# Attention with a running minimum, GpSimd adding the halves of pf, and evictions of 256 columns

## The chip, the cores and the metric

The kernel runs on one core of a Trainium2 chip. The metric is the device time of one execution in microseconds (us). A core has TensorE (PE; PEld is its weight load), VectorE (DVE), ScalarE (ACT), GpSimd (POOL) and SyncE (SP), which here issues nearly all DMA. Each works through its own instructions in order and waits on semaphores.

## The reference

One layer of a hybrid decoder on x of shape (1, 2048, 1024): an RMS norm, one input projection, three parallel branches (forgetting attention with 8 heads of 64, a Mamba-2 scan, a Griffin recurrence), each with a gate, and one output projection that is added to x. The change lies in the attention and in the output projection:

```python
q = rms_norm(q, q_g); k = rms_norm(k, k_g)
c = jnp.cumsum(log_f, axis=1)                       # per head
logits = einsum('bhqd,bhkd->bhqk', q_i, kt) * 64**-0.5 + (c_i[..., None] - ck[:, :, None, :])
logits = jnp.where(kpos[None, :] <= qpos[:, None], logits, -jnp.inf)
p = jax.nn.softmax(logits, axis=-1)
o = einsum('bhqk,bhkd->bhqd', p, vt)
...
mix = concatenate([y_att, y_ssd, y_lru], axis=-1)   # 512 + 1024 + 512
h = h + einsum('bse,ed->bsd', mix, w_out[l])
```

## The kernel before

All products are made of float32 values split into a high and a low part (names ending in h and l): three products of the parts, or two where one operand carries both parts in its 128 rows.

Up to about 1260 us the kernel normalises x, makes the projections and runs the state space and recurrent branches; q, k, v and the gates go to DRAM. In `group` p of q and k, line 804 scales q by the column `qg` of the constants `cv`, which line 294 multiplies by 0.125.

Then comes the attention. Its work is cut into 64 units (h, sb): a head and a block of 256 queries (two query tiles of 128). The heads 0 and 7 run sb from 7 down to 0, the others up. A unit has two halves:

- `logits` (L829 to L878): for each query tile and each chunk of up to 512 keys two products into S (L854, L855), then one VectorE instruction (L856) that writes L = S - cb, where cb is the cumulative sum of the keys, and keeps a running maximum mx. For the last chunk cb is replaced by cm, a masked copy that GpSimd makes (L849, two buffers). Then L859 negates mx on VectorE, and L860 is ScalarE's exp with bias mx, which also sums into sm. The page shows L856 as a custom instruction and a read of its accumulator, of 128x1.
- `attend` (L880 to L937): transposes T of L (L909), ScalarE's cast ph of T (L916), VectorE's remainder pl (L917), products O with v (L895, L896). v holds its two parts side by side, so O has two halves of 64 rows that must be added: O is copied to os (L929), transposed into pf (L933), and L934 on VectorE adds the halves of pf into ats, which is then multiplied by the gate zg (L935, GpSimd) and stored in at_d (L936). ats, os, zg have two buffers each; O and pf share two PSUM buffers.

The loop at the end interleaves the units: while unit i is attended, the logits of unit i + 1 are made. At every eighth unit (its third) the next but one head's keys, values and sums are loaded (`load_head`: cb 1 MB, kh twice 0.5 MB, vv 1 MB).

Between these, `fill` lets a generator `sweeps` run some steps as filler for TensorE. It makes the output projection in four sweeps over 16 row blocks t, two halves n of 512 columns each: `mix` loads the branch's block mt (L961, L963), casts it to mh (L964, ScalarE) and makes the remainder ml (L965, GpSimd); `half` makes 12 products into po (L977 to L979, four steps of three) and adds po to xr (L981, L983, VectorE). In the first two sweeps xr is loaded from x or from the partial sums pt_d (L996) and stored there again (L998), with two buffers; in the last two, xo takes its place. Before the first unit is attended, 12 steps of filler (three halves) are taken at once, after the logits of the first unit have been written (L1027 to L1033). During the attention po has one PSUM buffer; after it, from about 1920 us, five, and only the rest of the sweeps is left.

The order of the instructions on each engine is not that of the code: a scheduler arranges it by dependences and priorities. The logits of the first unit stand under `high_priority` and `issue_after`, which bring them up among the last projections.

Of the kernel before, what the change touches and what calls it, by code (L numbers as in the profile page):

```python
# [8 lines left out]
F32 = mybir.dt.float32  # L9
# [3 lines left out]
AF = mybir.ActivationFunctionType  # L13
ALU = mybir.AluOpType
AX = mybir.AxisListType
# [3 lines left out]
P = 128  # L19
# [11 lines left out]
FIRST = 12  # L31
# [16 lines left out]
def hybrid_block(ctx, tc, x, norm_g, w_in, q_norm_g, k_norm_g, forget_b, ssd_conv_w, ssd_conv_b,  # L48
# [8 lines left out]
    V, A, G, T = nc.vector, nc.scalar, nc.gpsimd, nc.tensor  # L57
# [142 lines left out]
    with tpool(name="p0", bufs=2) as p0, tpool(name="p01", bufs=1) as p01, \  # L200
# [71 lines left out]
        for tb in range(4):  # L272
            if tb + AHEAD < 4:
                norm_x(tb + AHEAD)
            for k in range(KD):
                pt, tag = ((psY, "Y"), (pst, "pt"))[(tb * KD + k) % 5 % 2]
                pt = pt.tile([P, 512], F32, name=f"pu{tb}_{k}", tag=tag)
                for i in range(4):
                    T.transpose(pt[:, i * P:(i + 1) * P],
                                xts[tb * 4 + i][:, k * P:(k + 1) * P], ident)  # L280
                g = ngc[:, k:k + 1]
                A.activation(uh[tb][k], pt, AF.Copy, scale=g)
                V.scalar_tensor_tensor(ul[tb][k], pt, g, uh[tb][k].bitcast(F32),
                                       op0=ALU.mult, op1=ALU.subtract)
            if tb == 0:
                pr = psY.tile([P, P], F32, name="pr2", tag="Y")
                T.transpose(pr, rows, ident)
                V.tensor_copy(cv, pr[:, 0:NV])


                j = CV["cw"]
                V.tensor_scalar(cv[:, j:j + 60], cv[:, j:j + 60], 0.5, None, op0=ALU.mult)
                j = CV["qg"]
                V.tensor_scalar(cv[:, j:j + 1], cv[:, j:j + 1], 0.125, None, op0=ALU.mult)
                j = CV["ba"]
                V.tensor_scalar(cv[:, j:j + 4], cv[:, j:j + 4], -1.0, None, op0=ALU.mult)
                j = CV["bx"]
                V.tensor_scalar(cv[:, j:j + 4], cv[:, j:j + 4], 0.5, None, op0=ALU.mult)
# [530 lines left out]
    def logits(h, sb):  # L829

        sm = a2.tile([P, 2], F32, name=f"sm{h}_{sb}", tag="sm")
        u = {"L": [], "sm": sm}
        steps = []

        def chunk(i, c0):
            kh, vv, cb, qh, ql = heads[h]
            u["vv"] = vv
            qt = sb * 2 + i
            n = (qt + 1) * P
            w = min(512, n - c0)  # L840
            if c0 == 0:
                u["L"].append(a4.tile([P, S], F32, name=f"L{h}_{qt}", tag="L"))
                u["mx"] = am.tile([P, 1], F32, name=f"mx{h}_{qt}", tag="mx")
            lt, mx = u["L"][i], u["mx"]
            last = c0 + w == n
            cc = cb[:, c0:c0 + w]
            if last:
                cm = a2.tile([P, 512], F32, name=f"cm{h}_{qt}", tag="cm")
                G.affine_select(out=cm[:, 0:w], in_=cc, pattern=[[-1, w]], compare_op=ALU.is_ge,  # L849
                                fill=-NEG, base=w - P, channel_multiplier=1)  # L850
                cc = cm[:, 0:w]
            qs = slice((sb % 2) * 256 + i * P, (sb % 2) * 256 + i * P + P)
            ps = psS.tile([P, 512], F32, name=f"S{h}_{qt}_{c0}", tag="S")
            T.matmul(ps[:, 0:w], qh[:, qs], kh[:, c0:c0 + w], start=True, stop=False)  # L854
            T.matmul(ps[:, 0:w], ql[:, qs], kh[:, c0:c0 + w], start=False, stop=True)  # L855
            V.tensor_tensor_reduce(lt[:, c0:c0 + w], ps[:, 0:w], cc, 1.0,  # L856
                                   -3.0e38 if c0 == 0 else mx, ALU.subtract, ALU.max, mx)
            if last:
                V.tensor_scalar(mx, mx, -1.0, None, op0=ALU.mult)  # L859
                A.activation(lt[:, 0:n], lt[:, 0:n], AF.Exp, bias=mx, accum_out=sm[:, i:i + 1])  # L860

        def first():
            j = units.index((h, sb))
            if j % 2 == 0 and j > 0:
                load_q(h, sb)
            za = a2.tile([P, 2, 64], F32, name=f"za{h}_{sb}", tag="za")
            u["za"] = za
            p, b = divmod(h, 2)
            dma(za, za_d[p][sb * 256:(sb + 1) * 256, b * 64:b * 64 + 64].rearrange(
                "(t p) c -> p t c", p=P))  # L870
            if j % 8 == 2 and h < 7:
                load_head(h + 1)

        steps.append(first)
        for i in range(2):
            for c0 in range(0, (sb * 2 + i + 1) * P, 512):
                steps.append(lambda i=i, c0=c0: chunk(i, c0))
        return u, steps  # L878

    def attend(h, sb, u, steps, fill):  # L880

        L, sm, vv, za = u["L"], u["sm"], u["vv"], u["za"]
        V.reciprocal(sm, sm)
        zg = a2.tile([P, 2, 64], F32, name=f"zg{h}_{sb}", tag="zg")
        for i in range(2):
            G.tensor_scalar(zg[:, i, :], za[:, i, :], sm[:, i:i + 1], None,
                            op0=ALU.mult)
        po = psO.tile([P, 256], F32, name=f"O{h}_{sb}", tag="O")
        nk = sb * 2 + 2

        def av(kp, ph, pl):
            for jj in range(2):
                kt = kp * 2 + jj
                ca = slice(P, 256) if kt == nk - 1 else slice(0, 256)
                T.matmul(po[:, ca], vv[:, kt, :], ph[:, jj, ca], start=(kt == 0), stop=False)  # L895
                T.matmul(po[:, ca], vv[:, kt, :], pl[:, jj, ca], start=False, stop=(kt == nk - 1))  # L896

        todo = None
        done = 0
        for kp in range(sb + 1):  # L900
            pt = psT.tile([P, 2, 256], F32, name=f"T{h}_{sb}_{kp}", tag="T")
            last = kp == sb
            ins = None
            for jj in range(2):
                kt = kp * 2 + jj
                for i in range(2):
                    if last and jj == 1 and i == 0:
                        continue
                    ins = T.transpose(pt[:, jj, i * P:(i + 1) * P], L[i][:, kt * P:(kt + 1) * P],  # L909
                                      ident)  # L910
            ph = a3.tile([P, 2, 256], F32R, name=f"ph{h}_{sb}_{kp}", tag="ph")
            pl = a3.tile([P, 2, 256], F32R, name=f"pl{h}_{sb}_{kp}", tag="pl")
            parts = [(slice(0, 2), slice(0, 256))] if not last else [
                (0, slice(0, 256)), (1, slice(P, 256))]
            for ja, ca in parts:
                A.copy(ph[:, ja, ca], pt[:, ja, ca])  # L916
                V.tensor_tensor(pl[:, ja, ca], pt[:, ja, ca], ph[:, ja, ca].bitcast(F32),  # L917
                                op=ALU.subtract)
            upto = len(steps) * (kp + 1) // (sb + 1)
            for st in steps[done:upto]:  # L920
                st()
            done = upto
            if todo is not None:
                av(*todo)
            todo = (kp, ph, pl)
            fill(ins)
        av(*todo)
        os_ = a2.tile([P, 256], F32, name=f"os{h}_{sb}", tag="os")
        A.copy(os_, po)  # L929
        pf = psO.tile([P, 256], F32, name=f"pf{h}_{sb}", tag="O")  # L930
        ats = a2.tile([P, 2, 64], F32, name=f"ats{h}_{sb}", tag="ats")
        for i in range(2):
            T.transpose(pf[:, i * P:(i + 1) * P], os_[:, i * P:(i + 1) * P], ident)  # L933
        V.tensor_reduce(ats, pf.rearrange("p (i u c) -> p i c u", i=2, u=2), axis=AX.X, op=ALU.add)  # L934
        G.tensor_tensor(ats, ats, zg, op=ALU.mult)  # L935
        dma(at_d[sb * 256:(sb + 1) * 256, h * 64:(h + 1) * 64].rearrange("(i p) c -> p i c", p=P),  # L936
            ats)  # L937
# [30 lines left out]
    def half(t, n, i, parts, xr):  # L968
# [5 lines left out]
        for j in range(4):  # L974
# [2 lines left out]
            T.matmul(ps, mh[:, j, :], h, start=(j == 0), stop=False)  # L977
            T.matmul(ps, mh[:, j, :], l, start=False, stop=False)  # L978
            T.matmul(ps, ml[:, j, :], h, start=False, stop=(j == 3))  # L979
        if kind in (0, 1):  # L980
            V.scalar_tensor_tensor(xr, ps, rsn[:, t, kind:kind + 1], xr, op0=ALU.mult, op1=ALU.add)  # L981
        else:
            V.tensor_tensor(xr, xr, ps, op=ALU.add)  # L983

    SEQ = ((12, "lru"), (8, 1), (4, 0), (0, "att"))

    def sweeps():
# [22 lines left out]
        for w, (t, i) in enumerate(work):  # L1010
# [13 lines left out]
                    dma(of[tsl, cs], xs[t][:, cs])  # L1024
            cur = nxt

    with tc.high_priority(offset=HP), tc.issue_after(anchor[1].ins):  # L1027
        cur, steps = logits(*units[0])
        for st in steps:
            st()  # L1030
    filler = sweeps()
    for _ in range(FIRST):
        next(filler)  # L1033
    count = [0, FIRST]
    recent = []

# [48 lines left out]
```

## Time and profile before

| what | value |
|---|---|
| median of 3 runs | 2093.52 us (2092.03 to 2095.52) |
| the profiled execution | 2093.96 us, span 2092.3 us |
| mean granted clock of TensorE | 0.986 |
| memory read, written | 168.22 MB, 94.57 MB |

In the rows of the profile, `out<-in` gives the tiles that an instruction writes and reads, L856 the line of the code. "busy" is the time in which an engine worked, "idle before" the time it stood still just ahead of these instructions, with what ended it behind the arrow. A row of waits reads "who waited <- for whom: us in total, times, longest". PEclk is the share of full speed at which TensorE's clock ran.

### The profile page before, as it was taken

The page shows a single profiled execution, that of the slowest core. Times are in us where ns is not written, and L with a number is a line of the kernel's source. Part 1 is how long each engine was busy: PE and PEld are TensorE (multiplying, and loading weights), DVE is VectorE, ACT ScalarE, POOL GpSimd, SP SyncE. Part 2 cuts the span into 40 slices and gives each one's busy share as a digit, 9 for nine tenths or more (in the row PEclk, how much of TensorE's full clock was granted, in tenths as well). Part 3 has the DMA queues.
Part 4 walks back from the last instruction along what each step waited for, and adds up shares of the span by engine and source line. Part 5 has one row for each costly group of instructions (what it writes and reads, how often), then busy time and mean ns, then how long its engine had stood idle before and what let it go on. Part 6 is the DMA issues. An engine that isn't in the chain of part 4 may idle for free. (4 is left out here: it accounts for less than half of the span.)

```text
span 2092.3 us, 35912 instructions
## 1 busy us (share of the span) xinstructions
PE 2008.3 (96%) x12485; PEld 1760.1 (84%) x12485; DVE 1261.7 (60%) x2720; ACT 956.7 (46%) x1989; POOL 540.6 (26%) x750
## 2 busy tenths in 40 slices
PE   7999999999999999998999998999999999999999
PEld 6788888887789998887888997978888888888887
DVE  6655555488874216767576255767777776884333
ACT  7444443466642214554444234555656555563010
POOL 0000001355531005454552001232223322212110
PEclk9999999999999999999999999999999999999999
DMA  5122233111123225666666647466466456342443
GB/s 195 41 71 61 71 112 96 39 42 42 42 72 95 83 81 161 189 186 201 193 163 177 163 147 218 135 175 164 128 178 187 126 151 155 116 142 78 136 137 120
DMA packets 287318, 265.18 MB, mean 127 GB/s; under 512 B 59780, under 2 KB 227232, under 8 KB 285088
## 3 DMA queue, kind: packets, MB, share of 16 engines
q1 hardware_dynamic: 286976, 262.85, 43.2%
q8 instruction: 99, 1.62, 0.3%
q14 instruction: 83, 0.68, 0.1%
q0 software_dynamic: 160, 0.03, 0.1%
HBM read 168.22 MB, written 94.57 MB: 126 GB/s over the span
## 5 line engine op out<-in xcount | busy, mean ns | idle before, releaser
L916 ACT CAST ph<-T 128x512 fp32r<-128x512 f32 (+2 forms) x352 | 163.4, 489 | 164.9 <-PE T L909 106.9
L917 DVE TENSOR_TENSOR pl<-T,ph 128x512 fp32r<-128x512 f32 (+2 forms) x352 | 192.7, 564 | 54.2 <-ACT ph L916 52.0
L977 PE MATMUL po<-woh,mh 128*128 128x512 f32 x512 | 215.3, 421 | 9.4 <-DVE xr L983 6.2
L978 PE MATMUL po<-wol,mh 128*128 128x512 f32 x512 | 202.9, 396 | 0.0
L979 PE MATMUL po<-woh,ml 128*128 128x512 f32 x512 | 201.3, 398 | 0.0
L860 ACT ACTIVATE L<-L,mx 128x1920 f32<-128x1920 f32 (+15 forms) x128 | 154.4, 1207 | 50.9 <-DVE mx L859 37.0
L909 PE MATMUL T<-ident,L 128*128 128x128 f32 x1088 | 173.0, 276 | 2.2 <-ACT L L860 2.0
L384 DVE SCALAR_TENSOR_TENSOR accx<-rtx,cv,accx 128x512 f32<-128x512 f32 x144 | 104.6, 752 | 90.8 <-ACT accx L381 76.3
L331 PE MATMUL pxx<-uh,wh 128*128 128x512 f32 x384 | 152.6, 400 | 5.4 <-ACT rtx L376 3.3
L895 PE MATMUL O<-ph,vv 128*128 128x256 f32 x576 | 154.4, 288 | 0.5 <-ACT ph L916 0.5
L896 PE MATMUL O<-pl,vv 128*128 128x256 f32 x576 | 152.0, 288 | 2.1 <-DVE pl L917 1.8
L332 PE MATMUL pxx<-ul,wh 128*128 128x512 f32 x384 | 153.7, 401 | 0.0
L319 PE MATMUL pqk<-wl,uh 128*128 128x256 f32 x512 | 152.7, 299 | 0.8 <-DVE wl L193 0.8
L333 PE MATMUL pxx<-uh,wl 128*128 128x512 f32 x384 | 152.8, 400 | 0.0
L318 PE MATMUL pqk<-wh,uh 128*128 128x256 f32 x512 | 147.1, 292 | 3.9 <-ACT wh L192 3.9
L320 PE MATMUL pqk<-wh,ul 128*128 128x256 f32 x512 | 149.2, 293 | 0.0
L319 PE MATMUL pzs<-wl,uh 128*128 128x256 f32 x512 | 144.8, 284 | 2.9 <-POOL wl L193 2.9
L849 POOL TENSOR_SCALAR_AFFINE_SELECT cm<-cb 128x384 f32<-128x384 f32 (+3 forms) x128 | 59.2, 465 | 336.9 <-DVE mx L856 190.2
L320 PE MATMUL pzs<-wh,ul 128*128 128x256 f32 x512 | 144.6, 284 | 0.0
L318 PE MATMUL pzs<-wh,uh 128*128 128x256 f32 x512 | 143.3, 283 | 0.0
L648 ACT ACTIVATE ab<-ab,nacs 128x128 f32<-128x128 f32 x256 | 82.6, 391 | 129.9 <-POOL ab L644 115.2
L854 PE MATMUL S<-kh,qh 128*128 128x512 f32 (+2 forms) x320 | 130.3, 408 | 10.8 <-DVE mx L856 10.1
(315 smaller groups left out, 5576.1 us busy)
## 6 DMA issues: line engine op xcount, KB each, us to landing
ab<-acs_d SPq DMA_DIRECT2D x64, 256.0 KB
pt_d<-xr SPq DMA_DIRECT2D x64, 256.0 KB
wr<-in_w_in_dram SPq DMA_DIRECT2D x192, 64.0 KB
wr<-in_w_in_dram SPq DMA_DIRECT2D x80, 128.0 KB
xt<-in_x_dram SPq DMA_DIRECT2D x16, 512.0 KB
xs_d<-stx SPq DMA_DIRECT2D x32, 256.0 KB
v_d<-vs SPq DMA_DIRECT2D x32, 256.0 KB
zs_d<-zs SPq DMA_DIRECT2D x32, 256.0 KB
```

Of the source, the lines that this page charges most:

```text
L318: T.matmul(ps[:, i, :], h[k][:, sl], wh[k], start=(k == 0), stop=False)
L319: T.matmul(ps[:, i, :], h[k][:, sl], wl[k], start=False, stop=False)
L320: ins = T.matmul(ps[:, i, :], l[k][:, sl], wh[k], start=False, stop=(k == KD - 1))
L332: T.matmul(ps, wh[k][:, ms], ul[tb][k], start=False, stop=False)
L860: A.activation(lt[:, 0:n], lt[:, 0:n], AF.Exp, bias=mx, accum_out=sm[:, i:i + 1])
L895: T.matmul(po[:, ca], vv[:, kt, :], ph[:, jj, ca], start=(kt == 0), stop=False)
L909: ins = T.transpose(pt[:, jj, i * P:(i + 1) * P], L[i][:, kt * P:(kt + 1) * P], ident)
L916: A.copy(ph[:, ja, ca], pt[:, ja, ca])
L917: V.tensor_tensor(pl[:, ja, ca], pt[:, ja, ca], ph[:, ja, ca].bitcast(F32), op=ALU.subtract)
L977: T.matmul(ps, mh[:, j, :], h, start=(j == 0), stop=False)
L978: T.matmul(ps, mh[:, j, :], l, start=False, stop=False)
L979: T.matmul(ps, ml[:, j, :], h, start=False, stop=(j == 3))
```

## The change

Four edits, and a move:

- the constant of q is -0.125, so S is the negative of what it was; L856 adds cb in place of subtracting it and keeps a minimum; exp takes scale -1 and the minimum as its bias; the negation L859 is left out;
- ScalarE copies pf to fs, a tile with os's tag (two buffers for both), and GpSimd adds the halves of fs into ats; VectorE's L934 is left out;
- the addition of po to xr is made in two instructions of 256 columns;
- the first 12 steps of the filler are taken one by one between the steps of the first unit's logits, under the same priority, and no longer after them.

```diff
-                V.tensor_scalar(cv[:, j:j + 1], cv[:, j:j + 1], 0.125, None, op0=ALU.mult)
+                V.tensor_scalar(cv[:, j:j + 1], cv[:, j:j + 1], -0.125, None, op0=ALU.mult)
...
             V.tensor_tensor_reduce(lt[:, c0:c0 + w], ps[:, 0:w], cc, 1.0,
-                                   -3.0e38 if c0 == 0 else mx, ALU.subtract, ALU.max, mx)
+                                   3.0e38 if c0 == 0 else mx, ALU.add, ALU.min, mx)
             if last:
-                V.tensor_scalar(mx, mx, -1.0, None, op0=ALU.mult)
-                A.activation(lt[:, 0:n], lt[:, 0:n], AF.Exp, bias=mx, accum_out=sm[:, i:i + 1])
+                A.activation(lt[:, 0:n], lt[:, 0:n], AF.Exp, bias=mx, scale=-1.0,
+                             accum_out=sm[:, i:i + 1])
...
-        V.tensor_reduce(ats, pf.rearrange("p (i u c) -> p i c u", i=2, u=2), axis=AX.X, op=ALU.add)
+        fs = a2.tile([P, 2, 2, 64], F32, name=f"fs{h}_{sb}", tag="os")
+        A.copy(fs.rearrange("p i u c -> p (i u c)"), pf)
+        G.tensor_tensor(ats, fs[:, :, 0, :], fs[:, :, 1, :], op=ALU.add)
         G.tensor_tensor(ats, ats, zg, op=ALU.mult)
...
-        if kind in (0, 1):
-            V.scalar_tensor_tensor(xr, ps, rsn[:, t, kind:kind + 1], xr, op0=ALU.mult, op1=ALU.add)
-        else:
-            V.tensor_tensor(xr, xr, ps, op=ALU.add)
+        for m in range(2):
+            a, b = xr[:, m * 256:(m + 1) * 256], ps[:, m * 256:(m + 1) * 256]
+            if kind in (0, 1):
+                V.scalar_tensor_tensor(a, b, rsn[:, t, kind:kind + 1], a, op0=ALU.mult, op1=ALU.add)
+            else:
+                V.tensor_tensor(a, a, b, op=ALU.add)
...
+    filler = sweeps()
     with tc.high_priority(offset=HP), tc.issue_after(anchor[1].ins):
         cur, steps = logits(*units[0])
-        for st in steps:
+        for j, st in enumerate(steps):
             st()
-    filler = sweeps()
-    for _ in range(FIRST):
-        next(filler)
+            for _ in range(FIRST * (j + 1) // len(steps) - FIRST * j // len(steps)):
+                next(filler)
```

In the changed code the lines stand a little lower: the logits' eviction is L857, exp L860, ph L917, pl L918, the copy fs L936, GpSimd's add L937 and gate L938, the store L939, the products po L980 to L982, the evictions L986 and L988, the load and the store of xr L1001 and L1003, cb, kh and vv still L721 to L724.

The order of the instructions, at three places. In the names below the first number after S, L, mx, cm is the head and the second the query tile; after ats, fs, pf, zg, sm the head and the block; after pl and T the head, the block and a group of keys; after xr the row block, the half and the sweep; cb, kh and vv carry the head.

VectorE at unit (3, 1), while the logits of (3, 3) are made, before:

```order
L859 TENSOR_SCALAR mx3_5_17591<-mx3_5_17591 128x1
L856 ISA L3_6_17669,mx3_6_17670<-S3_6_512_17679,cm3_6_17675,mx3_6_17670 128x384
L856 ISA mx3_6_17670 128x1
L856 ISA L3_7_17702,mx3_7_17703<-S3_7_0_17704,cb3_16450 128x512
L856 ISA mx3_7_17703 128x1
L859 TENSOR_SCALAR mx3_6_17670<-mx3_6_17670 128x1
L934 TENSOR_REDUCE ats3_1_17620<-pf3_1_17619 128x128
L883 RECIPROCAL sm3_2_17531<-sm3_2_17531 128x2
L856 ISA L3_7_17702,mx3_7_17703<-S3_7_512_17712,cm3_7_17708,mx3_7_17703 128x512
L856 ISA mx3_7_17703 128x1
L859 TENSOR_SCALAR mx3_7_17703<-mx3_7_17703 128x1
```

and in the changed kernel:

```order
L857 ISA L3_6_17695,mx3_6_17696<-S3_6_0_17697,cb3_16467 128x512
L857 ISA mx3_6_17696 128x1
L884 RECIPROCAL sm3_2_17556<-sm3_2_17556 128x2
L857 ISA L3_6_17695,mx3_6_17696<-S3_6_512_17705,cm3_6_17701,mx3_6_17696 128x384
L857 ISA mx3_6_17696 128x1
L918 TENSOR_TENSOR pl3_1_1_17600<-T3_1_1_17595,ph3_1_1_17599 128x128
L857 ISA L3_7_17727,mx3_7_17728<-S3_7_0_17729,cb3_16467 128x512
L857 ISA mx3_7_17728 128x1
L918 TENSOR_TENSOR pl3_2_0_17663<-T3_2_0_17657,ph3_2_0_17662 128x512
L988 TENSOR_TENSOR xr14_0_0_17683<-xr14_0_0_17683,po14_0_12_17685 128x256 x2
L857 ISA L3_7_17727,mx3_7_17728<-S3_7_512_17737,cm3_7_17733,mx3_7_17728 128x512
L857 ISA mx3_7_17728 128x1
```

The negations L859 and the add L934 are gone; the addition L988 of the output projection comes as two instructions of 256 columns.

GpSimd at the same place, before:

```order
L849 AFFINE_SELECT cm3_6_17675<-cb3_16450 128x384
L935 TENSOR_TENSOR ats2_7_17467<-ats2_7_17467,zg2_7_17283 128x128
L849 AFFINE_SELECT cm3_7_17708<-cb3_16450 128x512
L886 TENSOR_SCALAR zg3_1_17533<-za3_1_17489,sm3_1_17473 128x64 x2
L935 TENSOR_TENSOR ats3_0_17525<-ats3_0_17525,zg3_0_17475 128x128
L849 AFFINE_SELECT cm3_8_17796<-cb3_16450 128x128
L935 TENSOR_TENSOR ats3_1_17620<-ats3_1_17620,zg3_1_17533 128x128
L886 TENSOR_SCALAR zg3_2_17628<-za3_2_17552,sm3_2_17531 128x64 x2
L849 AFFINE_SELECT cm3_9_17838<-cb3_16450 128x256
```

and in the changed kernel:

```order
L849 AFFINE_SELECT cm3_8_17822<-cb3_16467 128x128
L938 TENSOR_TENSOR ats2_7_17490<-ats2_7_17490,zg2_7_17306 128x128
L887 TENSOR_SCALAR zg3_1_17558<-za3_1_17514,sm3_1_17498 128x64 x2
L937 TENSOR_TENSOR ats3_0_17548<-fs3_0_17551 128x128
L849 AFFINE_SELECT cm3_9_17864<-cb3_16467 128x256
L938 TENSOR_TENSOR ats3_0_17548<-ats3_0_17548,zg3_0_17500 128x128
L887 TENSOR_SCALAR zg3_2_17653<-za3_2_17577,sm3_2_17556 128x64 x2
L937 TENSOR_TENSOR ats3_1_17643<-fs3_1_17646 128x128
L938 TENSOR_TENSOR ats3_1_17643<-ats3_1_17643,zg3_1_17558 128x128
L887 TENSOR_SCALAR zg3_3_17763<-za3_3_17666,sm3_3_17651 128x64 x2
L849 AFFINE_SELECT cm3_10_17950<-cb3_16467 128x384
```

Each unit has one row more, the add L937; the masks cm3_8 and cm3_9 stand ahead of that of ats3_1, and cm3_10, which had three rows between itself and the gate of that unit, has two.

GpSimd at unit (0, 1), before:

```order
L965 TENSOR_TENSOR ml7_12_15472<-mt7_12_15473,mh7_12_15471 128x512
L849 AFFINE_SELECT cm1_6_15452<-cb1_14415 128x384
L935 TENSOR_TENSOR ats0_1_15189<-ats0_1_15189,zg0_1_15123 128x128
L886 TENSOR_SCALAR zg1_0_15261<-za1_0_15217,sm1_0_15195 128x64 x2
L849 AFFINE_SELECT cm1_7_15499<-cb1_14415 128x512
L935 TENSOR_TENSOR ats0_0_15253<-ats0_0_15253,zg0_0_15197 128x128
```

and in the changed kernel:

```order
L849 AFFINE_SELECT cm1_6_15461<-cb1_14417 128x384
L968 TENSOR_TENSOR ml7_12_15481<-mt7_12_15482,mh7_12_15480 128x512
L937 TENSOR_TENSOR ats0_1_15195<-fs0_1_15198 128x128
L849 AFFINE_SELECT cm1_7_15508<-cb1_14417 128x512
L938 TENSOR_TENSOR ats0_1_15195<-ats0_1_15195,zg0_1_15131 128x128
L887 TENSOR_SCALAR zg1_0_15269<-za1_0_15225,sm1_0_15203 128x64 x2
```

The mask cm1_7 stood behind the gate of ats0_1 and behind zg1_0; now it stands between the add and the gate.

SP's transfers at the start of the attention, before (pt_d is the DRAM tensor of the partial sums):

```order
L998 DMA pt_d_14055<-xr0_0_0_14125 128x512
L961 DMA mt3_12_14316<-lr_d3_105 128x128
L869 DMA za0_5_14411<-za_d0_83 128x2x64
L723 DMA kh1_14413<-kl_d0_75 64x2048
L724 DMA vv1_14414<-v_d0_79 128x16x128
L996 DMA xr1_0_0_14168<-in_x_dram 128x512
L998 DMA pt_d_14055<-xr0_1_0_14142 128x512
```

and in the changed kernel:

```order
L1001 DMA xr1_0_0_14155<-in_x_dram 128x512
L870 DMA za0_5_14413<-za_d0_83 128x2x64
L721 DMA cb1_14417<-c_d_98 128x2048
L722 DMA kh1_14415<-kh_d0_71 64x2048
L1003 DMA pt_d_14055<-xr0_1_0_14109 128x512
L723 DMA kh1_14415<-kl_d0_75 64x2048
L724 DMA vv1_14416<-v_d0_79 128x16x128
```

The load of xr1_0_0 stood behind kh1 and vv1 and stands now ahead of cb1, kh1 and vv1. The load of xr1_1_0 comes in the changed kernel six rows below the last one shown.

## The prediction

> **What bounds the kernel now.** The page comes first: TensorE is busy for 96% of the span, so what can be won lies in the few places where it stands still, or runs at a lower clock. The view by stretches finds them: the projections and state space part up to 1260 us, the start of the attention up to 1320, the attention, and from 1920 the last output products. Its columns are length, then busy time and instructions of each engine, granted clock and DMA.
>
> ```profile
> PE 2008.3 (96%) x12485; PEld 1760.1 (84%) x12485; DVE 1261.7 (60%) x2720; ACT 956.7 (46%) x1989; POOL 540.6 (26%) x750
> core 0: us, PE busy (x) PEld busy (x) DVE busy (x) ACT busy (x) POOL busy (x), PEclk, DMA share, GB/s
> 1260.00:1320.00 60.00, 51.98 (x320) 44.67 (x320) 34.46 (x86) 25.90 (x44) 10.52 (x16) 0.94 0.68 195
> 1320.00:1920.00 600.00, 577.97 (x3648) 503.80 (x3646) 445.91 (x1271) 346.66 (x697) 177.08 (x339) 0.99 0.52 145
> 1920.00:2092.30 172.30, 167.49 (x757) 137.02 (x756) 51.27 (x74) 17.37 (x29) 16.85 (x13) 0.99 0.39 130
> ```
>
> Every edit but one scale constant acts after 1260 us. There TensorE stands still for 8.0 us in the first stretch and 22.0 in the second. VectorE is busy for 445.9 of 600 us (74%), not full: what it costs TensorE is single waits. The view of waits between 1260 and 1925 us, TensorE first, then VectorE (total, times, longest):
>
> ```profile
> PE S L854 <- DVE mx L856: 10.1, 16, 2.2
> PE po L977 <- DVE xr L983: 6.2, 1, 6.2
> PE pf L933 <- DVE ats L934: 3.3, 1, 3.3
> PE T L909 <- ACT L L860: 2.0, 4, 0.7
> PE O L895 <- ACT ph L916: 0.5, 2, 0.3
> DVE ats L934 <- DMA at_d<-ats: 14.5, 4, 4.7
> DVE xr L983 <- DMA xr<-in_x_dram: 8.1, 1, 8.1
> DVE L L856 <- POOL cm L849: 1.1, 2, 0.6
> ```
>
> TensorE waits for VectorE nearly throughout, and VectorE itself stood twice for DMA: four times, 14.5 us, before the add L934, because its target ats (two buffers) was still being stored; once, 8.1 us, before an eviction whose xr had not arrived. VectorE works in order, so the logits' evictions stood behind both. One of the four, by the timeline, at unit (3, 1):
>
> ```profile
> 1534.00 0.15 DVE L859 TENSOR_SCALAR mx<-mx 128x1 f32<-128x1 f32 x1
> 1536.78 0.39 PE L855 MATMUL S<-kh,ql 128*128 128x512 f32 x1
> 1537.95 0.42 DVE L934 TENSOR_REDUCE ats<-pf 128x128 f32<-128x256 f32 x1 [3.80 <-DMA at_d<-ats]
> 1538.36 0.73 DVE L856 CUSTOM_DVE_ANT_0 L<-S,cm,mx 128x512 f32<-128x512 f32 x1
> ```
>
> The stretches around all of them, and behind three of them:
>
> ```profile
> 1296.00:1303.30 7.30, 1.09 (x10) 0.78 (x8) 0.75 (x2) 0.68 (x2) 0.00 (x0) 0.78 1.10 284
> 1303.30:1308.00 4.70, 4.70 (x14) 3.79 (x15) 2.36 (x7) 2.05 (x3) 1.47 (x3) 0.61 0.75 229
> 1370.00:1376.40 6.40, 3.07 (x21) 2.38 (x20) 1.68 (x7) 2.45 (x8) 1.66 (x3) 0.91 1.02 228
> 1376.40:1384.00 7.60, 7.60 (x33) 6.50 (x33) 5.42 (x20) 5.01 (x11) 3.59 (x9) 0.63 0.95 253
> 1459.00:1463.00 4.00, 2.58 (x13) 1.87 (x11) 1.16 (x5) 2.10 (x6) 1.10 (x3) 1.00 0.60 154
> 1534.00:1539.00 5.00, 3.16 (x18) 2.25 (x16) 1.20 (x6) 2.53 (x7) 0.48 (x2) 1.00 0.52 137
> 1690.00:1695.00 5.00, 2.87 (x16) 2.06 (x15) 1.83 (x8) 0.80 (x3) 0.77 (x3) 1.00 0.95 243
> 1695.00:1699.00 4.00, 3.54 (x9) 2.61 (x10) 3.96 (x13) 3.31 (x8) 1.17 (x3) 0.63 0.53 159
> ```
>
> Length less PE busy: 6.2 us of standstill at the start, and at the four waits 3.33, 1.42, 1.84 and 2.13, together 8.72. Behind the longer ones the clock is down: (1 - 0.61) x 4.7 = 1.8 us at the start, (1 - 0.63) x 7.6 = 2.81 and (1 - 0.63) x 4.0 = 1.48 behind the first and the fourth wait. So the four waits hold 8.72 + 4.29 = 13.0 us, the start 8.0.
>
> **The change part by part.** The prices, from the view by lines (count | busy us, mean ns | idle before):
>
> ```profile
> L859 DVE TENSOR_SCALAR mx<-mx 128x1 f32<-128x1 f32 x128 | 18.6, 148 | 1.3
> L934 DVE TENSOR_REDUCE ats<-pf 128x128 f32<-128x256 f32 x64 | 26.8, 419 | 23.4 <-DMA at_d<-ats 14.5 <-PE pf L933 5.2 <-PE O L896 1.7
> L929 ACT COPY os<-O 128x256 f32<-128x256 f32 x64 | 23.7, 371 | 43.3 <-PE O L896 42.7
> L935 POOL TENSOR_TENSOR ats<-ats,zg 128x128 f32<-128x128 f32 x64 | 30.3, 473 | 114.6 <-DVE ats L934 68.8 <-issue 21.0 <-DVE sm L883 11.6
> L917 DVE TENSOR_TENSOR pl<-T,ph 128x512 fp32r<-128x512 f32 x224 | 149.7, 686 | 50.6 <-ACT ph L916 49.1
> L917 DVE TENSOR_TENSOR pl<-T,ph 128x256 fp32r<-128x256 f32 x64 | 26.7, 418 | 1.1 <-ACT ph L916 0.5
> L981 DVE SCALAR_TENSOR_TENSOR xr<-po,rsn,xr 128x512 f32<-128x512 f32 x32 | 23.9, 746 | 7.8 <-PE po L979 4.7 <-DMA xr<-pt_d 2.6
> L805 DVE SCALAR_TENSOR_TENSOR stl<-ptq,cv,sth 128x256 fp32r<-128x256 f32 x64 | 30.6, 480 | 45.6 <-DMA ql_d<-stl 16.2 <-ACT sth L804 15.3 <-DMA kl_d<-stl 13.4
> ```
>
> *The add of pf leaves VectorE.* The rows of the section on the change show VectorE at the place of that timeline (ats3_1): the row that waited for the store is gone, and S3_6, S3_7 and the casts pl run on without it. The wait itself doesn't go: ats still has two buffers, and its writer is now GpSimd's L937. Behind that instruction stand, by GpSimd's rows there, its gate L938, zg3_3 and mask cm3_10; the masks up to cm3_9, and with them all that VectorE's rows take, are made ahead of it. At ats0_1, the first of the four waits, it is otherwise: mask cm1_7, which S1_7 needs, stands right behind the waiting add, as before it stood behind the gate that followed it.
>
> ScalarE's copy fs needs its buffer back from L937 of the unit before, so it meets the wait one unit later. So I count the three later places whole, 1.42 + 1.84 + 2.13 + 1.48 of clock = 6.9 us (at heads 2 and 5 one mask less stands ahead of the wait, still one more than S_7 needs), and of the first (3.33 + 2.81) half, 3.1: **-10.0**, with ends 0 (GpSimd or ScalarE passes every wait on) and -13.0.
>
> That the 1.5 us goes along rests on this trace: 2.1 us of standstill between 1690 and 1695 was followed by 0.63, 1.4 and 1.8 elsewhere by nothing. The Trainium skill (TensorE: Matmul & The Clock Gate, Part 1: The HAM clock gate) says that the clock halves after about 3.4 us without work in a free-running window. By that rule only the first of the four places has a standstill long enough, and the term would be -8.5; the trace has the drop at the fourth too, and I keep the row.
>
> The price of the move: ScalarE gets 64 copies of L929's form, 64 x 371 ns = 23.7 us, in a stretch where it is busy for 346.7 of 600 us; TensorE waited only 2.0 + 0.5 us for ScalarE. **+1.5**, ends 0 and 23.7. GpSimd gets 64 x 473 ns = 30.3 us (it is busy for 177.1 of 600), and each store of ats is issued 0.47 us later, ahead of the next xr in SP's order: **+0.5**, ends 0 and 30.
>
> *The negation goes.* 128 x 148 ns = 18.9 us of VectorE, and ScalarE's exp starts that much sooner after the last chunk. Together with L934, VectorE loses 18.9 + 26.8 = 45.7 us and gets 11.6 (next edit) here: 7% of its work. Of the 10.1 + 2.0 us that TensorE waited for logits and exp I take 2: **-2**, ends 0 and -6 (half of them). Sign and scale change no instruction's form.
>
> *Evictions by halves.* Two of 256 columns against one of 512: 2 x 418 - 686 = 150 ns more for the add, 2 x 480 - 746 = 214 for the scaled one; 64 of each are 23.3 us of VectorE. Half fall after 1920 us, where VectorE is busy for 51.3 of 172.3 us and five buffers of po cover them. The other 11.6 us fall where po has one buffer, so the next product waits that much longer; in the waits above TensorE stands there once for long, for the late xr. **+1**, ends 0 and 11.6.
>
> *The first filler steps between the logits of the first unit.* By SP's rows they bring the load of the third half's xr (xr1_0_0) ahead of head 1's cb, kh and vv, where it stood behind kh and vv; now the fourth, xr1_1_0, is the one behind them. In the trace of before:
>
> ```profile
> 1292.83 0.48 SPq L723 DMA_DIRECT2D kh<-kl_d  x1
> 1293.35 0.59 SPq L724 DMA_DIRECT2D vv<-v_d  x1
> 1294.14 3.92 SPq L996 DMA_DIRECT2D xr<-in_x_dram  x1
> 1302.55 0.69 DVE L983 TENSOR_TENSOR xr<-xr,po 128x512 f32<-128x512 f32 x1 [8.14 <-DMA xr<-in_x_dram]
> ```
>
> From the issue of kh to xr's use it took 9.7 us. The fourth half is due one half, 12 products and some attention work, later than the third: that covers part. I take half of the 8.0 us: **-4.0**, ends 0 and -8.0.
>
> Sum: -10.0 + 1.5 + 0.5 - 2 + 1 - 4.0 = **-13.0 us**. The profiled execution took 2093.96 us (2092.3 span and 1.7 around it), 0.4 above the median of 2093.52; so 2093.5 - 13.0 = 2080.5.
>
> **The rivals.** *All waits go.* The start keeps no wait, the four places none, VectorE's relief gives its 6: -13 - 8 - 6 = -27, 2066.5 us. For it: VectorE is the only engine that TensorE waited long for. Against: mask cm_7 behind L937, and the fourth xr behind vv.
>
> *The waits only change engines.* The same stores land as late; GpSimd stops, and masks, ml and fs stop behind it, at three or more of the four places; the fourth xr waits as the third did. Then the first and the last term are nothing, and -2 + 1 + 1.5 + 0.5 = +1 is left: 2093.5 + 1 = 2094.5. For it: the last column but one of the stretches shows DMA at 0.5 to 1.1 of its time there, which the change doesn't touch. Against: the masks ahead of the wait in the rows above, and only 1.1 us of VectorE waiting for cm.
>
> *ScalarE passes the copy on: slower.* The copy of pf waits for two transposes, these for the copy of O; in ScalarE's order the next unit's casts ph stand behind. If each of the 64 delays a cast for which TensorE has nothing else, that is 64 x 371 ns = 23.7 in place of 1.5: -13 - 1.5 + 23.7 = +9.2, 2102.7. It decides from (13 + 1.5 + 4.2) / 64 = 0.29 us a unit. For it: L929, the same kind of copy, let ScalarE stand for 43.3 us. Against: TensorE waited 0.5 us for ph in all.
>
> That the change isn't in the program is excluded by the rows.
>
> **How the numbers follow.** My forecast, -8 to -20, has 0.50; all waits gone 0.17; changed engines 0.22; slower 0.11. About 0.2%, 4.2 us, is what a measurement of this kernel can tell. Faster: 0.50 + 0.17 + 0.05 of the third case (a place or two gained) = 0.72; the other 0.17 are the same; slower 0.11. The range, 2066.5 to 2094.5, runs from the second case to the third, and with the bounds of the small terms between them; it leaves out the fourth, where ScalarE's or GpSimd's upper bound is paid.
>
> **What would show it.** Right: no wait of VectorE for at_d; GpSimd's L937 waits for it instead, some 14 us; TensorE over 584 us busy of the 600 from 1320 on; at units (2, 1), (3, 1) and (5, 1) no standstill and no drop of the clock, at (0, 1) a smaller one; a wait for the fourth xr of some 4 us. Wrong: VectorE waiting for cm by more than 5 us in all, TensorE for ph by more than 10, or an xr wait of 8 us as before.

## The result and the profile after

The changed kernel took 2076.69 us (median of 4, 2074.41 to 2078.72) against 2094.19 us of the kernel before beside it: ratio 0.9917, 95% interval 0.9900 to 0.9934, so 17.4 us less (14 to 21). The forecast was 2080.5 us. The profiled execution after has a span of 2072.7 us, 19.6 less than the one before.

First the page's line of busy times, then the view by stretches of the prediction:

```profile
PE 2002.1 (97%) x12485; PEld 1759.0 (85%) x12485; DVE 1246.1 (60%) x2656; ACT 975.9 (47%) x2053; POOL 568.9 (27%) x814
1260.00:1320.00 60.00, 53.37 (x335) 46.63 (x334) 36.85 (x92) 27.38 (x47) 11.48 (x17) 0.97 0.71 211
1320.00:1920.00 600.00, 588.40 (x3727) 514.56 (x3726) 426.23 (x1158) 367.43 (x764) 206.70 (x405) 0.99 0.53 149
```

In the 600 us TensorE now stands still for 11.6 us where it stood for 22.0, and VectorE is busy for 19.7 us less, ScalarE for 20.8 and GpSimd for 29.6 more. The waits from 1260 to 1925 us:

```profile
PE po L980 <- DVE xr L988: 4.7, 1, 4.7
PE po L980 <- DVE xr L986: 3.2, 1, 3.2
PE S L854 <- DVE mx L857: 2.8, 8, 1.1
PE O L896 <- ACT ph L917: 1.9, 4, 1.1
DVE xr L988 <- DMA xr<-in_x_dram: 4.9, 1, 4.9
POOL ats L937 <- DMA at_d<-ats: 17.4, 5, 6.4
```

No row of VectorE for at_d is left; GpSimd's add L937 waits for the same stores, five times. TensorE's wait for the logits' evictions fell from 10.1 to 2.8 us. The wait for xr stayed, for another xr, and there is one new one of 3.2 us. Before had one more wait for an xr, which the prediction's waits leave out:

```profile
PE po L977 <- DVE xr L981: 2.5, 1, 2.5
```

Where the time came from, by the view in seven stretches that hold each place with what follows it, before and then after:

```profile
1288.00:1320.00 32.00, 25.79 (x149) 22.39 (x148) 12.97 (x33) 11.12 (x20) 4.82 (x7) 0.89 0.71 187
1364.00:1394.00 30.00, 26.38 (x153) 22.30 (x152) 20.09 (x66) 16.83 (x43) 11.62 (x26) 0.89 0.80 204
1450.00:1475.00 25.00, 23.28 (x149) 19.94 (x148) 19.29 (x64) 14.68 (x33) 9.80 (x18) 1.00 0.63 178
1525.00:1550.00 25.00, 23.00 (x148) 19.57 (x147) 18.27 (x61) 13.96 (x34) 8.29 (x17) 1.00 0.53 152
1560.00:1616.00 56.00, 53.41 (x337) 47.05 (x336) 43.08 (x120) 36.08 (x74) 18.21 (x32) 0.97 0.65 188
1684.00:1710.00 26.00, 23.41 (x140) 19.80 (x140) 18.03 (x59) 13.48 (x30) 9.07 (x19) 0.93 0.60 170
1750.00:1775.00 25.00, 22.51 (x140) 20.13 (x139) 16.30 (x47) 12.17 (x29) 6.99 (x15) 0.93 0.79 171
```

```profile
1288.00:1320.00 32.00, 27.29 (x160) 23.66 (x159) 18.08 (x47) 13.28 (x24) 6.28 (x9) 0.95 0.79 222
1364.00:1394.00 30.00, 29.07 (x189) 25.13 (x188) 22.76 (x70) 21.36 (x55) 17.46 (x37) 1.00 0.77 202
1450.00:1475.00 25.00, 25.00 (x160) 21.94 (x159) 19.73 (x55) 16.20 (x33) 10.10 (x22) 1.00 0.53 150
1525.00:1550.00 25.00, 24.85 (x163) 21.84 (x163) 18.83 (x51) 17.33 (x35) 8.35 (x19) 1.00 0.59 171
1560.00:1616.00 56.00, 52.03 (x314) 44.34 (x313) 38.29 (x102) 32.88 (x71) 19.92 (x38) 0.97 0.63 175
1684.00:1710.00 26.00, 25.85 (x166) 22.67 (x165) 20.84 (x57) 16.95 (x36) 9.30 (x20) 1.00 0.63 185
1750.00:1775.00 25.00, 25.00 (x161) 21.93 (x161) 19.20 (x56) 17.77 (x39) 11.25 (x24) 1.00 0.59 169
```

The loss of a stretch is its length less TensorE's busy time, plus its length times (1 - granted clock): in the first row of after 4.7 + 0.05 x 32 = 6.3 us. So for both kernels and for some of the experiments below (us, one profiled execution each; the clock has two digits, so a loss is good to about 0.3):

| kernel | start, 1288 | (0,1), 1364 | (2,1), 1450 | (3,1), 1525 | 1560 | (5,1), 1684 | 1750 | sum |
|---|---|---|---|---|---|---|---|---|
| before | 9.7 | 6.9 | 1.7 | 2.0 | 4.3 | 4.4 | 4.2 | 33.3 |
| changed | 6.3 | 0.9 | 0.0 | 0.2 | 5.7 | 0.2 | 0.0 | 13.2 |
| add of pf alone | 10.0 | 1.2 | 0.2 | 0.0 | 8.7 | 0.1 | 1.4 | 21.5 |
| filler alone | 11.6 | 4.2 | 1.9 | 0.2 | 5.2 | 6.1 | 1.3 | 30.5 |
| before, four ats | 11.9 | 6.7 | 0.1 | 0.2 | 5.5 | 0.1 | 2.7 | 27.2 |
| add of pf, four ats | 9.8 | 0.2 | 0.2 | 0.0 | 9.0 | 0.3 | 1.2 | 20.7 |
| changed, old filler | 7.5 | 7.9 | 0.0 | 0.0 | 6.6 | 0.0 | 0.0 | 22.1 |
| changed, three xr | 0.6 | 6.6 | 0.0 | 0.2 | 1.4 | 0.2 | 0.0 | 8.9 |
| changed, four ats | 9.1 | 2.4 | 0.0 | 0.0 | 7.0 | 0.0 | 0.0 | 18.5 |

From before to changed the seven stretches lose 20.1 us less; the spans differ by 19.6. They are named by what waited in them before; the stretch of (0, 1) also holds (0, 0), the unit after it.

What TensorE itself waited for at the four places of before differs. At (3, 1) and (5, 1) it was a logits' eviction (2.0 and 2.2 us), at (2, 1) a cast's remainder pl (1.6 us). At (0, 1) it was the add L934: the transposes of the next unit need the PSUM buffer of pf, which L934 had not yet emptied:

```profile
PE pf L933 <- DVE ats L934: 3.3, 1, 3.3
1375.64 0.42 DVE L934 TENSOR_REDUCE ats<-pf 128x128 f32<-128x256 f32 x1 [4.72 <-DMA at_d<-ats]
```

In the changed kernel ScalarE's copy empties that buffer, and it doesn't itself wait for that store.

### The profile page after: what moved, and what is told of

The parts are those of the page before. It is cut to its first block, busy times and chain, and to the rows that moved or that the text cites. A ratio compares the mean times of both kernels' runs of the same rounds, so it can differ in the third digit from the quotient of the medians.

```text
span 2072.7 us, 36031 instructions
## 1 busy us (share of the span) xinstructions
PE 2002.1 (97%) x12485; PEld 1759.0 (85%) x12485; DVE 1246.1 (60%) x2656; ACT 975.9 (47%) x2053; POOL 568.9 (27%) x814
## 5 line engine op out<-in xcount | busy, mean ns | idle before, releaser
L918 DVE TENSOR_TENSOR pl<-T,ph 128x512 fp32r<-128x512 f32 (+2 forms) x352 | 191.1, 565 | 70.8 <-ACT ph L917 69.5
L980 PE MATMUL po<-woh,mh 128*128 128x512 f32 x512 | 213.0, 416 | 8.9 <-DVE xr L988 4.7
L917 ACT CAST ph<-T 128x512 fp32r<-128x512 f32 (+2 forms) x352 | 161.9, 490 | 122.6 <-PE T L910 84.9
L981 PE MATMUL po<-wol,mh 128*128 128x512 f32 x512 | 201.5, 394 | 0.0
L982 PE MATMUL po<-woh,ml 128*128 128x512 f32 x512 | 200.5, 397 | 0.0
L860 ACT ACTIVATE L<-L,mx 128x1920 f32<-128x1920 f32 (+15 forms) x128 | 154.5, 1208 | 39.7 <-DVE mx L857 35.2
L910 PEld LDWEIGHTS T<-ident,L 128*128 128x128 f32 x1088 | 127.4, 141 | 13.5 <-ACT L L860 5.4
```

Of the source, the lines that this page charges most:

```text
L860: A.activation(lt[:, 0:n], lt[:, 0:n], AF.Exp, bias=mx, scale=-1.0, accum_out=sm[:, i:i + 1])
```

## The experiments

Each was timed beside the kernel before. Theory A is the forecast's: VectorE standing for the store of ats was the loss. Theory B: what counts is VectorE's work. Theory C: each edit shifts the order, and the waits fall otherwise by chance.

**The add of pf alone.**

```diff
-        V.tensor_reduce(ats, pf.rearrange("p (i u c) -> p i c u", i=2, u=2), axis=AX.X, op=ALU.add)
+        fs = a2.tile([P, 2, 2, 64], F32, name=f"fs{h}_{sb}", tag="os")
+        A.copy(fs.rearrange("p i u c -> p (i u c)"), pf)
+        G.tensor_tensor(ats, fs[:, :, 0, :], fs[:, :, 1, :], op=ALU.add)
```

> The kernel before with the add of pf alone moved (ScalarE's copy fs, GpSimd's add). Theory A (VectorE standing for the store of ats was the loss): VectorE waits for at_d not at all, GpSimd some 15 us in its place, and the time falls by 8 to 11 us, over half of the 17.4 that the whole change gave. Theory B (what counts is VectorE's work, not the wait): 26.8 us of VectorE go here and 18.9 with the negation, so this gives 10 and the negation alone 7. Theory C (each edit changes the scheduler's order, and the waits fall otherwise by chance): no relation to the four places; the four edits alone do not add up to 17.

Measured: 2079.64 us, ratio 0.9928 (0.9908 to 0.9949), 15.1 us less. GpSimd waits 14.4 us for at_d, VectorE not at all, and the four (h, 1) places lose 1.5 us in place of 15.0. This edit carries most of the change. A gave 8 to 11: the measured size is above it, though the interval (10.7 to 19.3) just reaches it. Work is taken off VectorE here as well as the wait, so this run alone doesn't tell A from B.

**The negation alone.**

```diff
...
-                                   -3.0e38 if c0 == 0 else mx, ALU.subtract, ALU.max, mx)
+                                   3.0e38 if c0 == 0 else mx, ALU.add, ALU.min, mx)
             if last:
-                V.tensor_scalar(mx, mx, -1.0, None, op0=ALU.mult)
...
```

> The kernel before with q negated, minimum for maximum and L859 gone; nothing else. Theory A: the four waits of VectorE for at_d stay, some 14 us, and the time falls by 1 to 3 us. Theory B: 18.9 us less of VectorE's work give some 7 us, while the four waits stay. Theory C: the waits for at_d change in number or length although ats is untouched.

Measured: 2093.85 us, ratio 1.0000 (0.9982 to 1.0019). VectorE waits 16.1 us for at_d, six times in place of four. 18.9 us less of VectorE's work gave nothing that shows: against B, and at A's lower end (a gain of up to 3.8 us is inside the interval). That the number of waits changed although ats is untouched is the sign that C named.

**The evictions in halves alone.**

```diff
-            V.tensor_tensor(xr, xr, ps, op=ALU.add)
+        for m in range(2):
+            a, b = xr[:, m * 256:(m + 1) * 256], ps[:, m * 256:(m + 1) * 256]
...
+                V.tensor_tensor(a, a, b, op=ALU.add)
```

> The kernel before with the additions to xr made in two instructions of 256 columns; nothing else. Theory A: 23.3 us more of VectorE, of which about 1 us reaches the end: 0 to +2 us. Theory B: it costs in proportion to VectorE's work in the attention, 11.6 of 26.8: +4 us or more. Theory C: anything from -5 to +5, by the places where VectorE waits for DMA.

Measured: 2093.13 us, ratio 0.9998 (0.9981 to 1.0015). No cost that shows, against B (a cost of up to 3.1 us is inside the interval). The waits moved here too: in the profiled execution VectorE waits for at_d seven times, 17.3 us in all.

**The first filler steps alone.**

```diff
         for j, st in enumerate(steps):
             st()
-    filler = sweeps()
-    for _ in range(FIRST):
-        next(filler)
+            for _ in range(FIRST * (j + 1) // len(steps) - FIRST * j // len(steps)):
+                next(filler)
```

> The kernel before with the first 12 filler steps taken between the steps of the first unit's logits; nothing else. Theory A: the wait of 8.1 us for the third half's xr goes and a wait of some 5 us for the fourth takes its place (the whole change showed 4.9): -1 to -3 us up to the first unit's end, the rest as before. Theory C: the first unit's place is the same, but later waits change, by more than 3 us in all.

Measured: 2087.90 us, ratio 0.9977 (0.9964 to 0.9990), 4.8 us less. But not at the start. The waits of that kernel from 1260 to 1925 us:

```profile
PE po L977 <- DVE xr L983: 6.5, 1, 6.5
DVE xr L983 <- DMA xr<-in_x_dram: 6.7, 1, 6.7
DVE ats L934 <- DMA at_d<-ats: 16.2, 6, 4.9
```

TensorE waits for the fourth xr as long as it did for the third (6.2 us). The start lost 11.6 us; what was gained stands in the table at (0, 1), (3, 1) and 1750, and part of it was lost again at (5, 1), in sum 2.8 us less lost than before, of 4.8 by the runs. That is C for this edit.

The four edits alone give 15.1, 0, 0.4 and 4.8 us less, together 20 against the 17.4 of the whole change. C said that they would not add up; with some 3 to 4 us of noise on each, that can't be told.

**Four buffers of ats in the kernel before**, the add still on VectorE.

```diff
-        ats = a2.tile([P, 2, 64], F32, name=f"ats{h}_{sb}", tag="ats")
+        ats = a2.tile([P, 2, 64], F32, name=f"ats{h}_{sb}", tag="ats", bufs=4)
```

> The kernel before with four buffers of ats in place of two; the add of pf stays on VectorE. Theory A (the loss was VectorE standing for the store of ats): no wait for at_d is left and the time falls by 8 to 12 us, most of the 15.1 that moving the add gave. Theory B (VectorE's 26.8 us of work were the loss): 0 to -3 us, although the waits are gone. Theory C (order by chance): anything in between, with TensorE standing still at other places than (0, 1), (2, 1), (3, 1) and (5, 1).

Measured: 2084.26 us, ratio 0.9951 (0.9935 to 0.9967), 10.3 us less: A's number, with all of VectorE's work in place. At (2, 1), (3, 1) and (5, 1) next to nothing is lost any more, 7.7 us less by the table. The table's sum fell by 6.1 only, where the span fell by 9.9; the rest isn't located. At (0, 1) as much is lost as before, by another transfer. That kernel's timeline there, ScalarE and GpSimd (in brackets the idle time before, and what ended it):

```profile
1377.92 0.83 ACT L860 ACTIVATE L<-L,mx 128x640 f32<-128x640 f32 x1 [3.90 <-POOL zg L886]
1377.04 0.85 POOL L886 TENSOR_SCALAR zg<-za,sm 128x64 f32<-128x64 f32 x2 [4.10 <-DMA za<-za_d]
```

GpSimd waits for za; its zg reads sm, of which there are two buffers; exp, which writes the next sm, waits for zg; and TensorE stands for the exponentials to transpose, 3.4 us at that place:

```profile
PE T L909 <- ACT L L860: 6.3, 6, 3.4
```

**VectorE waits but does no add.**

```diff
         A.copy(fs.rearrange("p i u c -> p (i u c)"), pf)
+        V.memset(ats[:, 0, 0:1], 0.0)
         G.tensor_tensor(ats, fs[:, :, 0, :], fs[:, :, 1, :], op=ALU.add)
```

> The kernel with the add of pf alone moved, and one more instruction on VectorE for each unit that writes a single column of ats ahead of GpSimd's add, so that VectorE waits for the store again but does no add; the output is the same. Theory A: VectorE waits for at_d some 14 us again and most of the 15.1 us are lost: -1 to -5 us against before. Theory B: VectorE is still relieved of 64 x (419 - some 60 to 150) ns, so -10 to -14 us stay although it waits.

Measured: 2115.10 us, ratio 1.0097 (1.0070 to 1.0123): 20.3 us more than before, 35 more than without this one instruction. VectorE's waits, and the instruction itself:

```profile
DVE ats L936 <- DMA at_d<-ats: 53.1, 29, 5.4
L936 DVE MEMSET ats<- x64: 59/59/59, 1270.2 to 1928.7; 128x1 f32 x64
```

It works 64 x 59 ns = 3.8 us in place of the add's 26.8. Having no data to wait for, it stands early in VectorE's order and waits at 29 places, not at 4, so this is more than the wait put back. B falls: less work and much more time. By the two runs some two thirds of what VectorE stands for the store reach the end: 35 of 53.1 us here, 10.3 of the 14.5 that the four buffers took away. That is a ratio of totals, not a count place by place.

**The next head's loads spread over three units.**

```diff
-            if j % 8 == 2 and h < 7:
-                load_head(h + 1)
+            if 2 <= j % 8 < 5 and h < 7:
+                if j % 8 == 2:
+                    parts[h + 1] = load_head(h + 1)
+                parts[h + 1](j % 8 - 2)
```

> The kernel before with the loads of the next head's cb, kh and vv (2.5 MB, all at a head's third unit) spread over its third, fourth and fifth units; nothing else. If these loads are what holds the stores of ats back (theory A1): VectorE's waits for at_d fall from 14.5 us to under 5, the 8.1 us for xr too, and the time falls by 6 to 15 us with the add still on VectorE. If the stores are late by their own place in SP's order, or by other transfers (A2): the waits stay above 10 us and the time within 3 us of before.

Measured: 2093.65 us, ratio 0.9994 (0.9975 to 1.0014). VectorE's waits for at_d stay, 13.7 us in six places, and that for xr stays at 7.8. So A2 so far: that all these loads stand in one unit is not what makes the stores late. (They are 3 MB, 1 for cb, 1 for kh and 1 for vv, not the expected 2.5. And at a head's third unit it is the next head that is loaded, not the next but one, as the section on the kernel has it.)

**TensorE adds the halves.**

```diff
-            T.transpose(pf[:, i * P:(i + 1) * P], os_[:, i * P:(i + 1) * P], ident)
+            T.matmul(pf[:, i * 64:(i + 1) * 64], os_[:, i * P:(i + 1) * P], id2, start=True, stop=True)
...
-        G.tensor_tensor(ats, ats, zg, op=ALU.mult)
+        G.tensor_tensor(ats, fs, zg, op=ALU.mult)
```

> The changed kernel with the halves of O added by TensorE: the two transposes of os become two products with two stacked identities of 64 columns, so pf has 128 columns, ScalarE copies half as much and GpSimd's add goes. If ScalarE's and GpSimd's share of the change costs anything (my +1.5 and +0.5): -1 to -3 us against the changed kernel. If these two engines have room: 0. If the float32 product costs TensorE more than the transpose: up to +15 us (64 units x 2 x some 0.1 us).

Measured: 2188.46 us, ratio 1.0460 (1.0430 to 1.0489): 112 us worse than the changed kernel. From the first copy of O to the last product it took 767.1 us against 752.4, 14.7 more, near the upper bound. The products run as two instructions each, the transposes as one (the row of the changed kernel below):

```profile
L937 PE MATMUL pf<-id,os x256: 217/275/323, 1418.5 to 2015.0; 128*128 128x64 f32 x128
```

```profile
L934 PE MATMUL pf<-ident,os x128: 270/272/330, 1319.0 to 1900.9; 128*128 128x128 f32 x128
```

The rest was lost before the attention, from 800 us on, in code that this edit doesn't touch: the first copy of O comes 99.5 us later. The only thing new there is the constant of 64 columns. Stretch 900 to 1000 of this kernel, then of the changed one:

```profile
900.00:1000.00 100.00, 70.57 (x312) 46.42 (x312) 62.18 (x85) 44.69 (x133) 68.25 (x72) 0.83 0.62 182
```

```profile
900.00:1000.00 100.00, 91.90 (x661) 80.92 (x660) 70.26 (x124) 47.35 (x136) 49.97 (x53) 0.98 0.67 194
```

TensorE had half the instructions there: the later projections no longer ran beside the state space part. Why is open, and so this run doesn't say what ScalarE's and GpSimd's share costs.

**Three buffers of xr in the changed kernel.**

```diff
-                    xr = o2.tile([P, 512], F32, name=f"xr{t}_{n}_{i}", tag="xr")
+                    xr = o2.tile([P, 512], F32, name=f"xr{t}_{n}_{i}", tag="xr", bufs=3)
```

> The changed kernel with three buffers of xr in place of two; by SP's rows the third and the fourth half's loads now both stand ahead of head 1's cb, kh and vv. If the standstill of 4.7 us at the start is the fourth load behind these transfers, and the 3.2 us at 1597 a load of xr that waited for its buffer: both go, with the half clock behind the first, and the time falls by 5 to 9 us against the changed kernel, to 2068 to 2072. If the loads only share the same DMA time: 0 to -2 us, with a wait for xr of some 5 us as before.

Measured: 2068.74 us, ratio 0.9885 (0.9867 to 0.9903): 6.7 us better than the changed kernel, the best of all. Both of TensorE's waits for xr went, by the table 5.7 us at the start and 4.3 around 1597; in the stretch of (0, 1) 5.6 came back, at (0, 0). ScalarE and GpSimd there:

```profile
1376.69 1.04 ACT L860 ACTIVATE L<-L,mx 128x896 f32<-128x896 f32 x1 [4.66 <-POOL zg L887]
1374.57 0.45 POOL L937 TENSOR_TENSOR ats<-fs 128x128 f32<-128x128 f32 x1 [6.81 <-DMA at_d<-ats]
```

This is the forecast's rival of waits that change engines, at one place: zg stands behind the waiting add, exp behind zg, and TensorE stood for 3.1 us and had the half clock behind. The store it waits for is that of (0, 2), the unit two before it. SP issued it right behind vv:

```profile
1365.97 0.40 SPq L724 DMA_DIRECT2D vv<-v_d  x1
1366.50 3.95 SPq L939 DMA_DIRECT2D at_d<-ats  x1
```

In the changed kernel SP issued the same store ahead of vv, and GpSimd's add of (0, 0) waited 0.6 us for it:

```profile
1370.28 0.37 SPq L939 DMA_DIRECT2D at_d<-ats  x1
1371.14 0.37 SPq L870 DMA_DIRECT2D za<-za_d  x1
1371.60 1.66 SPq L724 DMA_DIRECT2D vv<-v_d  x1
```

**The filler back behind the first unit's logits in the changed kernel.**

```diff
-            for _ in range(FIRST * (j + 1) // len(steps) - FIRST * j // len(steps)):
-                next(filler)
+    for _ in range(FIRST):
+        next(filler)
```

> The changed kernel with the first filler steps back behind the first unit's logits; all else as changed. If this move is worth 4 us or more, as the forecast said and as the kernel with it alone showed (-4.8): 2080.5 to 2082. If it only moves the wait from the third xr to the fourth, as the traces of the first unit show (-0.2 to -1): 2076 to 2078.

Measured: 2080.59 us, ratio 0.9943 (0.9928 to 0.9957), 5.4 us worse than the changed kernel (the intervals overlap a little). The start lost 7.5 us against 6.3; the stretch of (0, 1) lost 7.9 against 0.9, with GpSimd's add of (0, 0) standing 7.7 us for a store issued behind vv, and exp 5.6 for zg. So the move reads as some 5 us both alone and here, each with 3 to 5 us of noise, but not at the start.

**Four buffers of ats in the changed kernel**, the edit as above.

> The changed kernel with four buffers of ats. GpSimd's 17.4 us of waiting for at_d go. If these cost nothing, as nobody waits for GpSimd then: within 2 us of the changed kernel, 2075 to 2079. If they still reach the end through masks, ml or fs: 3 to 6 us less, and TensorE's 0.8 us at (0, 1) goes with them.

Measured: 2077.87 us, ratio 0.9927 (0.9911 to 0.9942): as the changed kernel. GpSimd's 17.4 us of waiting cost nothing that shows: at the three later places neither kernel loses more than 0.2. The waits for other transfers moved again. In the table this kernel loses 5.3 us more, 2.8 of them at the start and 1.5 at (0, 1). So an edit that leaves the time as it was can still shift some 3 us at one place.

**Four buffers of ats and the add moved.** Both edits above, on the kernel before.

> The kernel before with four buffers of ats and the add of pf moved: no wait for at_d on any engine. The four buffers alone gave -10.4 us, moving the add alone -15.1. If moving the add gives more than the waits, by relieving VectorE of 26.8 us: -14 to -17 against before. If the difference between the two was chance of the order: -9 to -12, as with the four buffers alone.

Measured: 2077.22 us, ratio 0.9928 (0.9914 to 0.9941), 15.1 us less, as with the add alone. Of the 4.8 us beyond the four buffers alone the table shows most at one place, (0, 1): 0.2 us against 6.7. The start and 1750 lose 2.1 and 1.5 less, 1560 loses 3.5 more, and the three later places are as they were, so the gain isn't spread over VectorE's work. SP asked for the za that zg waits for at 1373.72 here and at 1375.65 there; that this is the whole of it wasn't tried.

## Why the forecast was right, and where it was off

- *The add leaves VectorE, -10.0, ends 0 and -13.0.* Right in mechanism, too small. The table's four places gave 6.0 + 1.7 + 1.8 + 4.2 = 13.7 us. The three later ones went whole, as counted; the first went nearly whole, where I took half. I reasoned there with the logits' eviction behind the mask, but TensorE stood for pf's PSUM buffer, and that wait went with L934, since ScalarE empties the buffer now. That nothing took its place is in part luck: GpSimd's adds of (0, 1) and (0, 0) waited only 1.5 and 0.6 us. The reason for the half, work behind GpSimd's waiting add, is real: with three xr, or with the old filler, it cost 5.6 and 7 us more, one unit later. I named mask cm1_7 as what would be held up; it was zg, and behind it exp, by way of sm's two buffers.
- *The half clock goes along.* Right: no drop is left at any of the four places.
- *ScalarE +1.5, GpSimd +0.5.* Nothing shows: TensorE's wait for ph rose from 0.5 to 1.9 us, that for exp fell from 2.0 to 1.5, and four buffers of ats gave the changed kernel nothing. The slower rival's condition, 0.29 us a unit (18.7 us in all), was not near.
- *The negation, -2.* Not seen: 0 (-3.8 to +4.0). -2 lies inside that, so a small gain from VectorE's relief is neither shown nor shut out.
- *The halves, +1.* Not seen: -0.4 (-4.0 to +3.1), which has room for +1.
- *The first filler steps, -4.0.* The size came out (3.4 us at the start in the table, 4.8 to 5.4 by the runs), the reason didn't: that is luck. "That covers part" failed: alone, the fourth xr let TensorE stand for 6.5 us, as the third had for 6.2. With two buffers of xr, the starts of the kernels in the table with the move lost 6.3, 9.1 and 11.6 us, of those without 7.5 to 11.9, and with the halves alone 4.9: no order in them. The 5 us came from places further on: in the changed kernel the stretch of (0, 1), with the move alone also (3, 1) and 1750. The order of SP's transfers was another there; why it came out as a gain both times is open.
- *Left out.* Two waits for an xr loaded from pt_d: that at 1760 went (4.2 us), one at 1597 came (1.4 more in its stretch). The waits of before had the first as 2.5 us for L981. For the second the trace of the changed kernel names no cause; that of the same kernel with four ats does, and three xr remove it:

```profile
DVE xr L986 <- DMA xr<-pt_d: 4.5, 2, 3.6
```

The forecast fell short by 4.4 us of the runs' 17.4, and by 7.1 of the table's 20.1, which holds one execution of each kernel. Of these 7.1, 3.7 lie at the four places, 3 are costs charged that don't show, 2.8 are the two waits left out; 2 of the negation and 0.6 of the filler go the other way.

The signs named ahead came out: no wait of VectorE for at_d, 17.4 us of GpSimd's (some 14 forecast), 588.4 us of TensorE busy in 600 (over 584), 4.9 us for the fourth xr (4), clean (2, 1), (3, 1), (5, 1).

## What to carry to other kernels

Price an engine's wait by what stands behind it in its order, not by the engine's load: an instruction of 0.4 us that waited for a store on VectorE cost 10 us, the same wait on GpSimd nothing, until something that ScalarE needed stood behind it there. More buffers of the tile whose transfer is late are the first thing to try (four ats in the kernel before gave 10.3 us, three xr in the changed one 6.7); the next step here, three xr with four ats, was not run. After such a fix look at the same place again: the next transfer that is late there takes over.

## What the runs showed of the hardware

The clock fell after shorter standstills than expected. In the thirteen kernels of this study other than the one with the stacked identities, TensorE stood for 2.03 us or longer 38 times between 1285 and 1930 us, and all 38 times the granted clock of the next 7 us was 0.53 to 0.78; after ones of 1.4 to 2.00 us it stayed at 1.00 in 8 of 10 cases. The kernel before, then the one in which VectorE waits (each the standstill, then what follows):

```profile
1537.16:1539.16 2.00, 0.00 (x1) 0.00 (x1) 1.17 (x5) 0.00 (x0) 0.65 (x2) 1.00 0.02 7
1539.16:1546.00 6.84, 6.84 (x42) 5.97 (x43) 5.74 (x17) 3.82 (x8) 2.37 (x6) 1.00 0.37 111
```

```profile
1527.06:1529.56 2.50, 0.00 (x0) 0.00 (x0) 0.74 (x3) 0.29 (x1) 0.00 (x0) 1.00 0.04 13
1529.56:1536.00 6.44, 6.44 (x32) 5.63 (x33) 5.08 (x19) 3.77 (x12) 2.41 (x4) 0.74 0.41 139
```

By these 38 values the clock costs another 1.5 to 3.3 us behind such a standstill ((1 - clock) x 7 us). It isn't a little lower for long but at half for a short time: in the kernel before it is 0.50 from 1300.1 to 1306.9 us, and from 1696.1 to 1699.5 behind (5, 1). In all 13 traces such a stage between 1285 and 1930 us lasts 3.4, 6.8 or 10.2 us.

The prediction weighed the rule of the Trainium skill (TensorE: Matmul & The Clock Gate, Part 1: The HAM clock gate), by which the clock halves after about 3.4 us without work in a free-running window. 17 of the 38 standstills were shorter than 3.4 us, and so was the first place's 3.33 that the prediction counted as long enough. So here the rule gives too little, and the rows decide.
